# The output projection of feed-forward 1: the second pass begun within the first, and gated tiles loaded from ScalarE's queue

## The chip, the cores and the metric

The kernel runs on one core of one Trainium2 chip. The core has a matrix engine (TensorE, PE), a vector engine (VectorE, DVE), an engine for functions of one operand (ScalarE, ACT), GpSimd (POOL) and SyncE (SP), which here only issues DMAs; ScalarE can issue DMAs as well. The metric is the time of one execution on the device in microseconds, as the median of several runs.

## The reference

One layer works on 512 latent tokens and 256 context tokens of 1024 values, in float32. What matters here is the first of its two feed-forwards and the modulation rows:

```python
mod = (sc @ w_mod[l] + b_mod[l]).reshape(-1, N_MOD, D_MODEL)      # nine rows of 1024 per stream
x = ada_out(x, swiglu(ada_in(x, mod, 0, norm_pre[l, 0]), ffn_w_in[l, 0], ffn_w_out[l, 0]), mod, 0, norm_post[l, 0], 0.5)
xc = ada_out(xc, swiglu(ada_in(xc, modc, 0, ...), ...), modc, 0, norm_post[l, 0], 0.5)
# swiglu: a, b = split(y @ w_in); (silu(a) * b) @ w_out, with w_out of 2816 x 1024
# ada_out: x + 0.5 * gate * rmsnorm(z, g);  ada_in: rmsnorm(x, g) * (1 + scale) + shift
```

After it come a mixer (mLSTM heads and pooling) and a second feed-forward on the latent tokens alone, whose gate is row 8 of the modulation.

## The kernel before

Each float32 product is done as three matmuls: both operands are split into a high and a low part (`split_w`: the cast by ScalarE, line 81 by its helper, the difference by VectorE, line 78), and high x high, low x high and high x low are added in PSUM (`mm3`, lines 97 to 99; `mm3p`, line 102, the same in program order). Tokens are six tiles of 128: two of context, four latent. The hidden width of 2816 is 22 row blocks of 128.

The first half of feed-forward 1 (`in_fast`, one call per row block) makes the gated tile of 128 x 768 of each row block and stores it in DRAM (`g_d`). Its normed input lies in `yh` and `yl`.

The output projection (`out_pass`) takes two passes of three token tiles (384 tokens) each, so that its sums, three tiles x two halves of 512 columns, fit six PSUM banks: four of `pa`, two of `pz`. In a pass a row block needs its weights (512 KB, from `ffn_w_out` through the ring `raw` of five buffers, split into two `win` tiles) and its gated tile (192 KB, from `g_d`, split in `q3` buffers). `prepare` does both, two row blocks ahead, and all loads are issued by SyncE. The last row blocks (`tail`: 2 in the first pass, 4 in the second) go over one token tile after the other, so that each tile's end (`done1` and `ada_tile`: squares of the sums by ScalarE, line 148; the product with the gate row by VectorE, line 175, which empties the bank; the residual, line 179; the store of x1, line 185; a second norm, lines 148 and 187) lies beside the matmuls of the next. `back` then transposes the normed rows (line 105) and writes them, split, into `yh` and `yl`; `Backs(lag)` holds it back by so many ticks. The second pass goes through the row blocks with the last four of the first pass first, whose weight tiles are still there.

The other modulation rows (blocks 2 to 8) are made by `mod_steps`, a generator with ten steps per block: eight that each load one weight tile of 512 KB and add it, times a scalar, into a sum on VectorE (line 678, one operation per stream), one empty one, and one that sums over partitions on TensorE (line 688) and stores the row (line 704). `filler(n)` takes n steps. `in_fast` calls its `tick` twice per row block, and three of four ticks take one step (27 in all); the passes take the rest. When block 4 is done, `begin_chain` loads the gate rows and columns.

The order within each engine's queue is fixed when the program is built: a planner takes the instructions by priority and readiness, `keep_in_program_order` (`pin`) holds some of them in the order in which the code names them, and `issue_after` puts a group behind an instruction. An engine does its queue in order.

## Time and profile before

| | us |
|---|---|
| median of 3 runs | 1173.79 (1169.68 to 1174.12) |
| the profiled execution | 1170.85 |
| its span, first to last instruction | 1169.1 |
| TensorE busy in it | 1111.0 |
| VectorE busy in it | 894.8 |
| ScalarE busy in it | 530.6 |

All times of instructions below count from the first instruction of the profiled execution. The output projection lies at about 376 to 590 us, the first half of feed-forward 1 before it, the mixer at 620 to 825 and feed-forward 2 from 825 to the end.

### The profile page before, as it was taken

What the parts mean: (1) busy time and instruction counts of PE and PEld (TensorE: products, weight loads), DVE (VectorE), ACT (ScalarE), POOL (GpSimd) and SP (SyncE); (2) the same over time, 40 slices, a digit from 0 to 9 for tenths busy, and PEclk for the clock granted to TensorE, in tenths of its full rate; (3) what the DMA queues carried; (4) which work ended last, traced back from release to release, by engine and by line L of the source; (5) the groups of instructions that cost most, each with busy time, mean ns of one, the idle gap of its engine ahead of it and who ended that gap; (6) DMA issues with size and microseconds to landing.
All of it is one profiled execution on the core that took longest, in us unless ns stands there. A gap on an engine that the chain in (4) does not pass through costs nothing.

```text
span 1169.1 us, 17262 instructions
## 1 busy us (share of the span) xinstructions
PE 1111.0 (95%) x6610; PEld 1004.8 (86%) x6610; DVE 894.8 (77%) x1315; ACT 530.6 (45%) x910; POOL 106.4 (9%) x139
## 2 busy tenths in 40 slices
PE   4999999999999999599899799999999999999996
PEld 3899999999998877478699687888999899999995
DVE  3798997898798676557445867875899898888865
ACT  4544333333333333464364556557665344444431
POOL 4000000000000000200122314412000000000001
PEclk9999999999999999799999899999999999999999
DMA  9933433643544887549623112134334333333321
GB/s 306 287 121 104 151 124 100 200 133 97 184 153 127 328 301 274 190 159 324 215 83 99 37 63 64 64 109 148 123 91 120 116 108 109 109 108 109 107 75 73
DMA packets 152673, 169.25 MB, mean 145 GB/s; under 512 B 7415, under 2 KB 125687, under 8 KB 152589
## 3 DMA queue, kind: packets, MB, share of 16 engines
q1 hardware_dynamic: 152540, 168.12, 44.6%
q8 instruction: 52, 0.85, 0.3%
q14 instruction: 33, 0.26, 0.1%
q10 hardware_dynamic: 48, 0.01, 0.0%
HBM read 153.12 MB, written 14.98 MB: 144 GB/s over the span
## 4 chain that ended last, share of the span: by engine, by line
PE 47%; DVE 6%; ACT 2%; DMA 1%; issue 1%; POOL 1%; SPq 0%; DVEq 0%; ACTq 0%; POOLq 0%
PE pa L102 9%; PE pa L98 7%; PE pa L99 7%; PE pa L97 7%; PE pz L102 4%; PE pz L97 3%; PE pz L98 3%; PE pz L99 3%; PE pt L102 3%; PE pt L105 1%; DVE wins L78 1%; DMA raw<-in_w_in_dram 1%; ACT junk L148 1%; DMA q<-g 0%; DVE z L179 0%
## 5 line engine op out<-in xcount | busy, mean ns | idle before, releaser
L97 PE MATMUL pa<-yh,wins 128*128 128x256 f32 (+1 forms) x768 | 236.2, 308 | 0.7 <-ACT yh L81 0.4
L99 PE MATMUL pa<-yl,wins 128*128 128x256 f32 (+1 forms) x768 | 235.9, 307 | 0.0
L98 PE MATMUL pa<-yh,wins 128*128 128x256 f32 (+1 forms) x768 | 235.8, 307 | 0.0
L78 DVE TENSOR_TENSOR wins<-raw,wins 128x1024 fp32r<-128x1024 f32 (+1 forms) x144 | 156.6, 1087 | 70.5 <-PE pa L98 39.8
L81 ACT CAST wins<-raw 128x1024 fp32r<-128x1024 f32 (+1 forms) x146 | 136.2, 935 | 110.5 <-PE pa L99 36.9
L97 PEld LDWEIGHTS pa<-yh,wins 128*128 128x128 f32 x768 | 145.0, 189 | 3.0 <-issue 0.8
L99 PEld LDWEIGHTS pa<-yl,wins 128*128 128x128 f32 x768 | 144.9, 189 | 0.5
L98 PEld LDWEIGHTS pa<-yh,wins 128*128 128x128 f32 x768 | 144.9, 189 | 0.5
L99 PE MATMUL pa<-tl,wins 128*128 128x384 f32 (+1 forms) x388 | 122.3, 315 | 0.0
L98 PE MATMUL pa<-th,wins 128*128 128x384 f32 (+1 forms) x388 | 121.8, 314 | 0.0
L97 PE MATMUL pa<-th,wins 128*128 128x384 f32 (+1 forms) x388 | 121.3, 313 | 0.0
L678 DVE SCALAR_TENSOR_TENSOR m<-m,sc,m 128x1024 f32<-128x1024 f32 x80 | 100.2, 1278 | 9.6 <-DMA m<-in_w_mod_dram 5.9
L81 ACT CAST wins<-sw 128x1024 fp32r<-128x1024 f32 x78 | 81.7, 1047 | 48.9 <-PE pa L99 35.5
L78 DVE TENSOR_TENSOR wins<-sw,wins 128x1024 fp32r<-128x1024 f32 x78 | 95.2, 1221 | 10.7 <-PE pa L98 7.0
L102 PE MATMUL pa<-yh,wins 128*128 128x512 f32 (+2 forms) x352 | 97.0, 362 | 0.0
L97 PEld LDWEIGHTS pa<-th,wins 128*128 128x128 f32 x388 | 72.8, 188 | 0.9 <-issue 0.8
L99 PEld LDWEIGHTS pa<-tl,wins 128*128 128x128 f32 x388 | 73.0, 188 | 0.1
L98 PEld LDWEIGHTS pa<-th,wins 128*128 128x128 f32 x388 | 73.0, 188 | 0.0
L102 PEld LDWEIGHTS pa<-yh,wins 128*128 128x128 f32 x352 | 62.0, 191 | 9.2 <-issue 2.2
L97 PE MATMUL pa<-wins,q 128*128 128x512 f32 x148 | 55.3, 407 | 8.9 <-ACT q L81 8.9
L102 PE MATMUL pa<-yl,wins 128*128 128x512 f32 (+2 forms) x176 | 62.4, 355 | 0.5 <-DVE yl L78 0.5
L98 PE MATMUL pa<-wins,q 128*128 128x512 f32 x148 | 59.3, 400 | 1.2 <-DVE q L78 1.2
(388 smaller groups left out, 2177.1 us busy)
## 6 DMA issues: line engine op xcount, KB each, us to landing
raw<-in_ffn_w_in_dram SPq DMA_DIRECT2D x87, 512.0 KB
raw<-in_ffn_w_out_dram SPq DMA_DIRECT2D x62, 512.0 KB
m<-in_w_mod_dram SPq DMA_DIRECT2D x57, 512.0 KB
g<-q SPq DMA_DIRECT2D x22, 384.0 KB
q<-g SPq DMA_DIRECT2D x44, 192.0 KB
raw<-in_w_in_dram SPq DMA_DIRECT2D x16, 512.0 KB
raw<-in_w_mod_dram SPq DMA_DIRECT2D x11, 512.0 KB
raw<-in_w_out_dram SPq DMA_DIRECT2D x16, 256.0 KB
```

Source lines behind the costliest of these rows:

```text
L78: return eng.tensor_tensor(out=out_ap, in0=a, in1=b, op=ALU.subtract)
L81: return S.copy(hi, src)
L97: T.matmul(out_ap, lhsT=wh, rhs=xh, start=first, stop=False, **kw)
L98: T.matmul(out_ap, lhsT=wl, rhs=xh, start=False, stop=False, **kw)
L99: T.matmul(out_ap, lhsT=wh, rhs=xl, start=False, stop=last, **kw)
L102: return tc.keep_in_program_order(T.matmul(*args, **kw))
L105: return tc.keep_in_program_order(T.transpose(**kw))
L148: return S.activation(out=junk, in_=src, func=AF.Square, scale=D ** -0.5, accum_out=ssq)
L678: V.scalar_tensor_tensor(out=accs[st], in0=w, scalar=sc[:, st * KD + k:st * KD + k + 1], in1=accs[st], op0=ALU.mult, op1=ALU.add)
```

## The change

- `out_pass` becomes a class. `fetch` loads a gated tile, from ScalarE's queue, and is pinned; `prepare` loads and splits the weights and splits the gated tile. Tiles are fetched five to six row blocks ahead and prepared two ahead, as before.
- `first.start(1)` prepares the first row block before the last call of `in_fast`. `second.start(4)` fetches and prepares four row blocks of the second pass after the last row block of the first pass is prepared and before its tail.
- The second pass multiplies its first four row blocks (`head`) for one token tile after the other.
- Ten weight tiles are kept for the second pass: four in `win` as before, six more in the space of `yh` and `yl`, which is free until `back` writes. For that the ticks by which `back` is held rise from 4 to 14. The second pass starts with these ten.
- The store of x1 and those of the modulation rows are issued by ScalarE; the store in `ada_tile` comes after the square of the second norm.
- `mod_steps` takes its blocks and buffers as arguments, and loads the norm's gains ahead of the weights of a block. From the 17th tick on every tick of `in_fast` takes a step (32 steps in all); the first pass takes one in every second row block, the second one in each of its first 18.
- Block 8 is made in feed-forward 2, one step per call of `in_fast` there, with `raw` buffers for its weights.

```diff
--- before.py
+++ after.py
@@ -166,7 +166,7 @@
     x1_d = [dpool.tile([P, D], F32, name=f"x1_{t}") for t in range(4)]
     x2_d = [dpool.tile([P, D], F32, name=f"x2_{t}") for t in range(4)]
 
-    def ada_tile(t, zs, z, halves, xr, gc, store, nxt, junk, half, keep=lambda ins: ins):
+    def ada_tile(t, zs, z, halves, xr, gc, store, nxt, junk, half, keep=lambda ins: ins, put=load):
 
 
         r = rstd2(halves)
@@ -181,9 +181,9 @@
                 load(store[:, cs], z[:, cs])
         if nxt is None:
             return None
+        r2 = rstd1(z, junk)
         if store is not None:
-            load(store, z)
-        r2 = rstd1(z, junk)
+            put(store, z)
         V.tensor_scalar_mul(xr, z, r2)
         scale, shift = nxt
         ts = slice(t * P, (t + 1) * P)
@@ -386,7 +386,9 @@
             qd = pa()
             product(qd, uh[:, lo], ul[:, lo], "t3")
             V.tensor_add(u3, u2, qd[:, 0:n])
-            self.tick(V.tensor_add(cb[:, n:2 * n], u3, p5))
+            end = V.tensor_add(cb[:, n:2 * n], u3, p5)
+            if self is f1:
+                self.tick(end)
             qe = pa()
             product(qe, x22p[:, lo], x22p[:, hi], "t4")
             V.tensor_add(cb[:, 0:n], u3, qe[:, 0:n])
@@ -472,7 +474,7 @@
             st = 1 if t < 2 else 0
             load(xr, ctxt[t * P:(t + 1) * P, :] if t < 2 else x[(t - 2) * P:(t - 1) * P, :])
             return ada_tile(t, qs, z, halves, xr, chain["g"][st], None if t < 2 else x1_d[t - 2], chain["y"][st], junk,
-                            lambda: q3()[:, 0:512], pin)
+                            lambda: q3()[:, 0:512], pin, nc.scalar.dma_start)
 
         blocks1 = ((0, 384), (384, 384))
         f1 = Ffn(ffn_w_in[0], ffn_w_out[0], range(NTT), 0, NT)
@@ -664,47 +666,53 @@
             S.mul(wqk, kc(p), float(P) ** -0.5)
 
 
-        def mod_steps():
-            for blk, streams in ((2, (0, 1)), (3, (0, 1)), (4, (0, 1)), (5, (0,)), (6, (0,)), (7, (0,)), (8, (0,))):
+        def mod_steps(blocks, new, acc, ahead):
+            for blk, streams in blocks:
                 accs = {}
+                j, ty = divmod(blk, 3)
+
+                nq = 4 // len(streams)
+                n = D // nq
+                at = [(st, i, 32 * (nq * st + i), slice(i * n, (i + 1) * n)) for st in streams for i in range(nq)]
+
+                def gains():
+                    gb = new()[:, 0:n]
+                    src = norm_pre if ty == 1 else norm_post
+                    for st, i, g, cs in at:
+                        load(gb[g:g + 32], src[j:j + 1, cs].broadcast_to([32, n]))
+                    return gb
+
                 for st in streams:
-                    accs[st] = m4()
+                    accs[st] = acc()
                     G.memset(accs[st], 0.0)
                     load(accs[st][0:1, :], b_mod[blk:blk + 1, :])
+                res = gains() if ty and ahead else None
                 for k in range(KD):
-                    w = m4()
+                    w = new()
                     load(w, w_mod[k * P:(k + 1) * P, blk * D:(blk + 1) * D])
                     for st in streams:
                         V.scalar_tensor_tensor(out=accs[st], in0=w, scalar=sc[:, st * KD + k:st * KD + k + 1],
                                                in1=accs[st], op0=ALU.mult, op1=ALU.add)
                     yield
                 yield
-
-                nq = 4 // len(streams)
-                n = D // nq
-                at = [(st, i, 32 * (nq * st + i), slice(i * n, (i + 1) * n)) for st in streams for i in range(nq)]
                 p = pt()[:, 0:n]
...
-                res = m4()[:, 0:n]
                 if ty == 0:
+                    res = new()[:, 0:n]
                     S.copy(res, p)
                 else:
-                    gb = m4()[:, 0:n]
-                    src = norm_pre if ty == 1 else norm_post
-                    for st, i, g, cs in at:
-                        load(gb[g:g + 32], src[j:j + 1, cs].broadcast_to([32, n]))
-                    V.scalar_tensor_tensor(out=res, in0=p, in1=gb, op1=ALU.mult,
+                    res = res if ahead else gains()
+                    V.scalar_tensor_tensor(out=res, in0=p, in1=res, op1=ALU.mult,
                                            **(dict(scalar=1.0, op0=ALU.add) if ty == 1 else
                                               dict(scalar=1.0 if j == 1 else 0.5, op0=ALU.mult)))
                 for st in streams:
                     rows[(blk, st)] = dpool.tile([1, D], F32, name=f"row{blk}_{st}")
                 for st, i, g, cs in at:
-                    load(rows[(blk, st)][:, cs], res[g:g + 1])
+                    nc.scalar.dma_start(rows[(blk, st)][:, cs], res[g:g + 1])
                 yield blk
 
-        steps = mod_steps()
+        steps = mod_steps([(b, (0, 1)) for b in (2, 3, 4)] + [(b, (0,)) for b in (5, 6, 7)], m4, m4, True)
 
         def filler(n):
             for _ in range(n):
@@ -734,67 +742,110 @@
         count = iter(range(100))
 
         def mod_tick(ins):
-            if next(count) % 4 < 3:
+            i = next(count)
+            if i % 4 < 3 or i > 16:
                 with tc.issue_after(ins.ins):
                     filler(1)
 
         f1.tick = mod_tick
-        for f in range(4, NF):
-            f1.in_fast(f)
-
 
         wos = {}
 
-        def out_pass(half, order, tail, homes, z, xr, before, backs):
...
+        class OutPass:
+            def __init__(self, half, order, head, tail, homes):
+                self.half, self.order, self.head, self.tail, self.homes = half, order, head, tail, homes
+                self.g, self.raws = {}, {}
+
+            def fetch(self, f):
+
+                self.raws[f] = q3()[:, 0:384]
+                pin(nc.scalar.dma_start(self.raws[f], g_d[f][:, 384 * self.half:384 * self.half + 384]))
+
+            def prepare(self, f):
                 if f not in wos:
                     r = raw()
                     load(r, f1.wo_ap[f * P:(f + 1) * P, :])
...
+                    wos[f] = split_w(r, to=self.homes[f]() if f in self.homes else None, keep=pin)
                 g = q3(F32R)
...
+                self.g[f] = split_w(self.raws[f], to=(g[:, 0:384], g[:, 384:NT]), keep=pin)
+
+            def start(self, n):
+
+                self.loaded, self.ready = iter(self.order), iter(self.order)
+                for f in self.order[:n]:
+                    self.fetch(next(self.loaded))
+                for f in self.order[:n]:
+                    self.prepare(next(self.ready))
+                self.n = n
+
+            def more(self, i):
+                if i + 5 >= self.n:
+                    for f in [next(self.loaded, None) for _ in range(max(1, 6 - self.n if i == 0 else 1))]:
+                        if f is not None:
+                            self.fetch(f)
+                if i + 2 >= self.n:
+                    for f in [next(self.ready, None) for _ in range(3 - self.n if i == 0 else 1)]:
+                        if f is not None:
+                            self.prepare(f)
+
+            def product(self, f, j, h, mm3):
+                (gh, gl), (wh, wl) = self.g[f], wos[f]
+                ts, cs = slice(j * P, (j + 1) * P), slice(512 * h, 512 * h + 512)
+                mm3(self.qs[j][h], gh[:, ts], gl[:, ts], wh[:, cs], wl[:, cs], f == self.order[0], f == self.order[-1])
+
+            def run(self, z, xr, before, backs, fill, then=lambda: None):
+                order, head, tail = self.order, self.head, self.tail
+                self.qs = [(pa(), pa()), (pa(), pa()), (pz(), pz())]
+                for i in range(head):
+                    self.more(i)
+                for j in range(3):
+                    for f in order[:head]:
+                        for h in range(2):
+                            self.product(f, j, h, mm3)
+                for i in range(head):
+                    before.tick()
+                for i, f in enumerate(order[:-tail]):
+                    if i >= head:
+                        self.more(i)
+                        for j in range(3):
+                            for h in range(2):
+                                self.product(f, j, h, mm3)
+                        before.tick()
+                    filler(fill(i))
+                for i in range(len(order) - tail, len(order)):
+                    self.more(i)
+                then()
+                for j in range(3):
+                    t, halves = 3 * self.half + j, small(2)
                     for h in range(2):
...
+                        for f in order[-tail:]:
+                            self.product(f, j, h, mm3p)
+                        square_to(halves[:, h:h + 1], self.qs[j][h], junk[:, 512 * h:512 * h + 512])
+                        backs.tick()
+                    backs.add(done1(t, self.qs[j], z[:, j], halves, xr(j)))
 
...
-        backs, first_backs = Backs(4), Backs(4)
+        first = OutPass(0, list(range(NF)), 0, 2, {0: lambda: (m4(F32R), m4(F32R))})
+        for f in range(4, NF):
+            if f == NF - 1:
+                first.start(1)
+            f1.in_fast(f)
+
+        backs, first_backs = Backs(4), Backs(14)
         xr1 = rows3("tl")
         order = list(range(NF))
-        out_pass(0, order, 2, {0: lambda: (sw(F32R), sw(F32R))}, rows3("th"), lambda i: xr1[:, i], Backs(0), first_backs)
-        for f in order[:-4]:
+
+        kept = order[-10:-4]
+        places = [y.rearrange("p k c -> p (k c)")[:, i * D:(i + 1) * D] for i in range(6) for y in (yh, yl)]
+        homes = {f: lambda i=i: (places[2 * i], places[2 * i + 1]) for i, f in enumerate(kept)}
+        first.homes.update(homes)
+        order = order[-10:] + order[-11::-1]
+        second = OutPass(1, order, 4, 4, {})
+        first.run(rows3("th"), lambda i: xr1[:, i], Backs(0), first_backs, lambda i: i % 2, lambda: second.start(4))
+        for f in order[10:]:
             wos.pop(f)
-        order = order[-4:] + order[-5::-1]
         homes = {order[-4]: lambda: (sw(F32R), sw(F32R))}
         late = []
 
@@ -805,7 +856,8 @@
             return late.pop(0)
 
         homes.update({order[-3]: late_home, order[-2]: late_home})
-        out_pass(1, order, 4, homes, rows3("tl"), lambda i: m4(), first_backs, backs)
+        second.homes.update(homes)
+        second.run(rows3("tl"), lambda i: m4(), first_backs, backs, lambda i: 1)
 
 
         wv = []
@@ -1317,13 +1369,23 @@
         pool = sx.enter_context(tc.tile_pool(name="ffn2", bufs=6, reuse_waits="tile"))
         sums = sx.enter_context(tc.tile_pool(name="sums2", bufs=1, reuse_waits="tile"))
         junk = pool.tile([P, D], BF16, name="junk3", bufs=1)
-        gc2 = pool.tile([P, D], F32, name="gc2", bufs=1)
-        bc_row(gc2, (8, 0))
+
+        def row_tile():
+            return pool.tile([P, D], F32, tag="gc2", name="gc2", bufs=1)
+
+        late = mod_steps([(8, (0,))], raw, row_tile, False)
+        gains2 = []
+
+        def last_row(ins):
+            if not gains2:
+                with tc.issue_after(ins.ins):
+                    if next(late, None) == 8:
+                        gains2.append(bc_row(row_tile(), (8, 0)))
 
         def done2(t, z, halves):
             xr = raw()
             load(xr, x2_d[t - 2])
-            return ada_tile(t, [z[:, 0:512], z[:, 512:1024]], z, halves, xr, gc2, out[(t - 2) * P:(t - 1) * P, :], None, junk, None)
+            return ada_tile(t, [z[:, 0:512], z[:, 512:1024]], z, halves, xr, gains2[0], out[(t - 2) * P:(t - 1) * P, :], None, junk, None)
 
         f2.scope(pool, done2, lambda: None, junk)
 
@@ -1352,7 +1414,7 @@
         f2.wo = {f: f2.out_weights(f, f) for f in range(2)}
         f2.w[2] = f2.last_sums(first)
         rest()
-        f2.fast = True
+        f2.fast, f2.tick = True, last_row
         f2.run(lambda f: ((NCTX, NLAT),), started=(0, 1))
```

## Rows read from the trace of the kernel before

**Rows 1.** The page: busy us, share of the span and instructions of each engine.
```profile
PE 1111.0 (95%) x6610; PEld 1004.8 (86%) x6610; DVE 894.8 (77%) x1315; ACT 530.6 (45%) x910; POOL 106.4 (9%) x139
```

**Rows 2.** Busy us by stretch (counts), then TensorE's clock, DMA share and GB/s.
```profile
376.00:575.00 199.00, 180.88 (x799) 142.97 (x799) 126.51 (x144) 82.79 (x136) 12.46 (x22) 0.95 0.73 259
465.00:470.00 5.00, 4.83 (x15) 3.87 (x16) 2.55 (x4) 1.38 (x4) 0.39 (x2) 0.67 1.02 401
480.00:485.00 5.00, 0.00 (x0) 0.00 (x0) 4.26 (x7) 4.07 (x10) 1.64 (x4) 0.50 0.04 14
485.00:490.00 5.00, 3.16 (x7) 2.05 (x8) 3.14 (x4) 1.10 (x4) 2.07 (x3) 0.50 0.92 274
505.00:555.00 50.00, 50.00 (x227) 40.28 (x226) 33.99 (x38) 26.25 (x41) 0.00 (x0) 1.00 0.80 279
```

**Rows 3.** Timeline, TensorE, second pass: start, us, engine, line, operation.
```profile
546.59 0.39 PE L97 MATMUL pa<-wins,q 128*128 128x512 f32 x1
554.81 0.39 PE L97 MATMUL pa<-wins,q 128*128 128x512 f32 x1
```

**Rows 4.** Timeline, first pass's tail: start, us; in brackets idle before, releaser.
```profile
461.31 0.85 PE L102 MATMUL pa<-wins,q 128*128 128x512 f32 x3
462.35 1.05 ACT L81 CAST wins<-raw 128x1024 fp32r<-128x1024 f32 x1 [3.70 <-DMA raw<-in_ffn_w_out_dram]
465.18 6.30 PE L102 MATMUL pa<-wins,q 128*128 128x512 f32 x20 [0.81 <-DVE q L78]
471.31 2.94 PE L102 MATMUL pz<-wins,q 128*128 128x512 f32 x12
```

**Rows 5.** Timeline, seam between the passes.
```profile
476.12 0.63 PE L105 MATMUL pt<-ident,tlz 128*128 128x128 f32 x4 [1.87 <-DVE tlz L187]
481.41 1.28 DVE L175 TENSOR_TENSOR thz<-pz,m 128x512 f32<-128x512 f32 x2
484.03 0.34 SPq L185 DMA_DIRECT2D x<-thz  x1
484.48 0.38 SPq L759 DMA_DIRECT2D q<-g  x1
485.10 0.50 ACT L81 CAST q<-q 128x384 fp32r<-128x384 f32 x1
485.64 1.65 PE L97 MATMUL pa<-wins,q 128*128 128x512 f32 x3 [8.90 <-ACT q L81]
492.35 0.40 PE L97 MATMUL pz<-wins,q 128*128 128x512 f32 x1
```

**Rows 6.** Timeline, second pass's tail; last row from the chain of work.
```profile
561.41 0.34 SPq L759 DMA_DIRECT2D q<-g  x1
563.74 0.51 ACT L81 CAST q<-q 128x384 fp32r<-128x384 f32 x1 [9.25 <-DMA q<-g]
568.01 0.84 PE L102 MATMUL pa<-sw,q 128*128 128x512 f32 x3
584.79 5.48 PE pz L102 x24
```

**Rows 7.** Two lines' instructions: least, median, most ns, and starts.
```profile
L678 DVE SCALAR_TENSOR_TENSOR m<-m,sc,m x80: 1272/1278/1285, 112.8 to 541.6; 128x1024 f32<-128x1024 f32 x80
L759 SPq DMA_DIRECT2D q<-g x44: 319/384/1433, 362.6 to 564.3; - x44
```

**Rows 8.** Busy time by stretch, two row blocks of feed-forward 1's first half.
```profile
141.00:155.70 14.70, 14.70 (x86) 14.70 (x85) 14.56 (x19) 5.64 (x9) 0.00 (x0) 1.00 0.43 134
155.70:170.40 14.70, 14.70 (x86) 14.70 (x85) 12.12 (x17) 5.59 (x9) 0.00 (x0) 1.00 0.37 117
```

**Rows 9.** Busy time by stretch, feed-forward 2; SyncE's waits 850:1000 (us, times, longest).
```profile
850.10:936.90 86.80, 85.32 (x612) 80.11 (x611) 81.70 (x123) 42.92 (x65) 0.00 (x0) 1.00 0.36 108
936.90:1029.70 92.80, 92.80 (x650) 87.05 (x650) 79.95 (x122) 40.05 (x61) 0.00 (x0) 1.00 0.36 107
SPq L114 <- DVE wos L78: 43.2, 9, 11.3
```

More of the change, by code (lines that the diff above doesn't have):

```diff
@@ L768, in out_pass @@
-            for f in order[:2]:
-                prepare(f)
-            for f, later in zip(order[:-tail], order[2:]):
-                prepare(later)
-                for i in range(3):
-                    for h in range(2):
-                        product(f, i, h, mm3)
-                before.tick()
-                filler(2 if half == 0 and f % 3 == 0 else 1)
-            for f in order[len(order) - tail + 2:]:
-                prepare(f)
-            for i in range(3):
-                t, halves = 3 * half + i, small(2)
-                for h in range(2):
-                    for f in order[-tail:]:
-                        product(f, i, h, mm3p)
-                    square_to(halves[:, h:h + 1], qs[i][h], junk[:, 512 * h:512 * h + 512])
-                    backs.tick()
-                backs.add(done1(t, qs[i], z[:, i], halves, xr(i)))
+                self.g[f] = split_w(self.raws[f], to=(g[:, 0:384], g[:, 384:NT]), keep=pin)
```

13 lines of the change are left out of this document (removed).

## Prediction

> **What bounds the kernel now.** I read the page's busy times first. TensorE is busy for 1111.0 of 1169.1 us [rows 1], so almost all of the time is matmuls that the change doesn't remove, and only the 58 us in which TensorE is idle, and the stretches at a low clock, can be won. The granted clock and the busy time by stretch come next. The output projection of feed-forward 1 lies at 376 to about 590 us; in its first 199 us TensorE is busy for 180.88, at a mean clock of 0.95 of full speed, and around it there are long stretches without any idle time. Last I read the order of time around each hole. There are three, and each can be priced against the undisturbed pace: 36 matmuls of 512 columns lie between the starts 546.59 and 554.81, so one takes 0.228 us [rows 3].
>
> **Hole A, the tail of the first pass.** It runs from 461.31 to 474.25 (471.31 + 2.94), 12.9 us for 3 tiles x 2 halves x 2 row blocks x 3 = 36 matmuls, which at 0.228 are 8.2 us. Lost: 4.7 us. The wait is for a split on ScalarE that itself waited for a weight load (3.70 us, released by the DMA) [rows 4]; the clock then reads 0.67 in 465 to 470, between its two levels of 1.2 and 2.4 GHz, after the idle time [rows 2].
>
> **Hole B, the seam between the passes.** From 474.25 to 492.35, 18.1 us, TensorE does four transposes (0.6) and 12 matmuls (2.7). Lost: 14.8 us. The reader is to see a chain of queues: SyncE issues the store of the first latent tile (x<-thz) only at 484.03, and the next load of a gated tile (q<-g) only right behind it at 484.48; ScalarE's first split for the new pass is at 485.10, and TensorE, idle for 8.90 us, starts at 485.64 [rows 5]. DMA share in 480 to 485 is 0.04, so nothing is short of bandwidth there; and in 485 to 490 the clock is 0.50, its lower level, after those 9 us without a matmul [rows 2].
>
> **Hole C, the tail of the second pass.** From 568.01 to 590.27 (584.79 + 5.48), 22.3 us for 3 x 2 x 4 x 3 = 72 matmuls, which are 16.4 us. Lost: 5.8 us. The load of a late gated tile is issued at 561.41 only, and ScalarE has stood idle for 9.25 us when it arrives [rows 6].
>
> A + B + C = 25.3 us. This is what the change can win.
>
> **The change part by part.**
>
> Gated tiles through ScalarE's queue, five to six row blocks ahead, and the store of x1 and of the modulation rows there as well. This takes out of SyncE's queue just the store that held the load at 484.48. The 44 loads cost SyncE 0.384 us each in the median, at most 1.43 [rows 7]; ScalarE now pays that. In 505 to 555, twelve row blocks of 4.1 us, ScalarE is busy for 26.25 of 50 us, so 2.2 per row block, with 1.9 free [rows 2]; 0.38 fits. Bounds: from nothing to 1.43 per row block, which still fits. I take nothing. What is queued behind an issue on ScalarE are the casts of the following weights and tiles, two row blocks (8 us) ahead of TensorE.
>
> Here the Trainium skill speaks against the change. Its page "DMA: Bandwidth & Descriptors", section "Issuing engines are not separate DMA queues", says that transfers started from different engines end on the same 16 DMA engines and interleave, so that spreading them saves issue time alone. By it, hole B would stay but for issue time; the share of 0.04 in the hole says that B is order, not bandwidth, so there I go by the row. For A and C it is the first rival.
>
> Second pass begun tile by tile. The first four row blocks of the second pass are loaded and split before the first pass's tail, and are multiplied for one token tile after the other: 24 matmuls, 5.5 us, for each tile. The third tile's banks come free last, at 482.69 (481.41 + 1.28), 8.4 us after the tail's end; before, each row block went over all three tiles, so the first one already needed them. Now they are needed only after 11 us. VectorE is freer in this stretch too, since fewer modulation steps lie in it. So B goes, but for a margin of 2.6 us that I don't trust fully: residue 1 us, bounds 0 and 7.4 (half of it).
>
> Ten weight tiles kept instead of four. The second pass loads and splits 12 instead of 18 blocks of 512 KB. Of the modulation loads, 8 remain in the first pass (21 before) and 14 in the second (12 before), counted from the steps. Over the stage that is 17 loads, 8.9 MB, less than the 51.5 MB (259 GB/s x 199 us [rows 2]) of now, and 6.8 MB of it leave the first pass, at whose end hole A is a late load. A goes; of C I leave 2 us, as a row's store now waits in ScalarE's queue shortly before the last splits (bounds 0 and 5.8).
>
> The y tiles of the first three token tiles are written later, after the kept weights in their place were used; transposes and casts are the same in number and lie beside matmuls. Free.
>
> More modulation steps in feed-forward 1's first half (32 instead of 27). Five steps of two VectorE operations of 1.278 us [rows 7] are 12.8 us on VectorE. A row block with two of them per tick pair (four operations) has VectorE at 14.56 of 14.70 us, one with two operations at 12.12, and TensorE at 14.70 in both [rows 8]. So a full row block fits, with 0.14 us to spare, but so far every second one was a light one; now three and then four full ones follow each other. Bounds 0 and 12.8; I take 0.5, as the nearest row shows no wait at the same load.
>
> The last gate row (block 8) moves into feed-forward 2: eight weight tiles of 512 KB through the ring of five raw buffers, and eight operations of 1.28 us on VectorE, one per row block from 850 us on. From 850.1 to 936.9 VectorE is busy for 81.70 of 86.80 us: 5.1 us free, and seven operations are 8.9 us, so 3.8 are missing; from there on it has 12.8 us free in 92.8 [rows 9]. SyncE already waits long for raw buffers there (43.2 us in nine waits for one line alone) [rows 9]. Even at this load TensorE was busy for 85.32 of the 86.80 us, so VectorE has some lead and part of the lack is hidden. Bounds 0 and 10.2 (all eight on the path); I take 3. What is late next is the split of the next row block's weights, which queues behind the new operation, and TensorE waits for that. The skill's page "Perfetto Trace Analysis", section "Identifying the Most-Contended Engine", takes occupancy as a fair measure of how near VectorE is to its limit; with 94% in the row it names VectorE as the engine to spare here. By that rule all that is missing, 3.8 us, would show, instead of the 3 I take.
>
> **Sum.** The profiled execution took 1170.85 us (span 1169.1). 1170.85 - 25.3 + 1 (B) + 2 (C) + 0.5 + 3 = 1152.1. That execution lies 2.9 us below the median of the three runs (1173.79) and inside their range; a median of the changed kernel may lie as much above it, so I put 1153.
>
> **Rivals.**
>
> First: the tails are short of bandwidth, and the queue doesn't matter. For it: DMA share 1.02 in 465 to 470 [rows 2]. Against: holes at 0.04. Then A and C shrink only with the bytes, by 17%: of 10.5 us 8.7 stay. 1170.85 - 14.8 - 1.8 + 1 + 3.5 = 1158.8. Chance 0.15.
>
> Second: the seam doesn't close, the change doesn't do there what it says. ScalarE's queue is in order, and the four early tiles' splits may stand in it behind the squares of the first pass's last tiles, or the third tile's banks come more than 2.6 us later than before. Then half of B stays: 1170.85 - 25.3 + 7.4 + 2 + 3.5 = 1158.5. Chance 0.14.
>
> Third: feed-forward 2 pays in full, and the ring of raw buffers with it: 10.2 instead of 3, so 1159.3, and with a late load for every third row block of about 2 us some 1165. For it: the 94% above. Against: after 936.9 VectorE has room. Chance 0.10.
>
> Fourth, on the other side: ScalarE is held by the loads that it now issues. A load that has to wait for its buffer or for a place in the queue stops the casts behind it. From 1.9 us per row block it stretches the row block of 4.1 us; at 2.3 us on each of 44 the 18.7 us of the sum are gone, at 2.8 it costs 44 x 0.9 = 40 us, so 1152.1 + 40 = 1192. For it: one issue took 1.43 us. Against: the median of 0.384, and ten buffers for some eight tiles alive. Chance 0.05.
>
> **How the numbers follow.** Forecast 0.54, the four rivals 0.15, 0.14, 0.10 and 0.05; 0.02 for several of the costs together that leave no change. About 0.5% (5.9 us) is what a measurement of this kernel can tell from none. Faster by more than that, below 1167.9: forecast, first and second rival, and most of the third, 0.88, less 0.02 for their upper ends, 0.86; within it 0.08; slower 0.06. The range: at the low end all 25.3 us are won and nothing is paid, 1145.5, and 1 us for the runs, so 1144; at the high end the first three rivals with their outer ends, 1165.
>
> **What would show it.** In the trace after: no idle time above 1 us and a clock of 1.0 between the last tail matmul of the first pass and the second pass; tail matmuls at 0.23 us in both tails; loads q<-g in ScalarE's queue and no stretched ScalarE; TensorE fully busy from 230 to 370; 0 to 4 us of waits for VectorE in the first eight row blocks of feed-forward 2. I would be wrong if holes of the same sum appear elsewhere, or if a full row block of feed-forward 1 grows beyond 14.7 us.

## The result, and the profile after

The changed kernel takes 1159.83 us (median of 4 runs, 1159.06 to 1162.81), the kernel before 1172.84 us beside it: a ratio of 0.9898, 95% interval 0.987 to 0.9925. The profiled execution took 1160.3 us, with a span of 1158.6; before it was 1170.85 and 1169.1.

The page of the changed kernel, busy us, share of the span and instructions (as [rows 1]):

```profile
PE 1107.9 (96%) x6610; PEld 1002.4 (87%) x6610; DVE 886.3 (76%) x1309; ACT 522.9 (45%) x904; POOL 104.6 (9%) x139
```

The number of matmuls is the same; the span is 10.5 us shorter. To see where, I cut both executions at the same five instructions: the tick (line 379) of row block 19 of feed-forward 1, the first matmul of the first tail, that of the second tail, the first matmul after the projection, and the first and last tick of feed-forward 2. All times in us:

| stretch | before | after | change |
|---|---|---|---|
| start to the tick of row block 19 | 335.64 | 336.54 | +0.9 |
| to the first tail | 125.67 | 128.63 | +3.0 |
| first tail and second pass | 106.70 | 86.59 | -20.1 |
| second tail | 22.45 | 22.47 | 0.0 |
| mixer, to feed-forward 2's first tick | 259.62 | 260.41 | +0.8 |
| feed-forward 2, first to last tick | 282.38 | 286.32 | +3.9 |
| to the end | 36.64 | 37.64 | +1.0 |

The gain lies in one row, holes A and B; 4.7 us of it are hole A, as the first tail now takes 8.2 us (465.17 to 473.41) instead of 12.9. Hole C stayed, a new hole came ahead of the first tail, and feed-forward 2 grew.

**The seam.** Busy time by stretch after (columns as in [rows 2]), and the matmuls and the third tile's banks there:

```profile
473.40:480.00 6.60, 6.60 (x31) 5.46 (x30) 4.18 (x7) 2.89 (x8) 2.43 (x6) 1.00 0.01 1
480.00:490.00 10.00, 10.00 (x46) 8.28 (x45) 5.45 (x8) 3.14 (x6) 2.26 (x5) 1.00 0.55 174
```

```profile
465.17 5.66 PE L102 MATMUL pa<-wins,q 128*128 128x512 f32 x24
...
473.41 0.39 PE L97 MATMUL pa<-yh,q 128*128 128x512 f32 x1
...
479.75 1.28 DVE L175 TENSOR_TENSOR thz<-pz,m 128x512 f32<-128x512 f32 x2
...
482.53 0.33 ACTq L186 DMA_DIRECT2D x<-thz  x1
482.89 1.31 ACTq L762 DMA_DIRECT2D q<-g  x2
```

Where [rows 5] had 8.90 us without a matmul, the second pass now follows the tail at its own pace, with kept weights from the space of `yh`, at a clock of 1.00. The store of x1 still waits for the third tile, and a load still stands right behind it, now on ScalarE; but the tiles that the second pass begins with were loaded and split long before.

**Ahead of the first tail.** VectorE, TensorE and one issue of SyncE around the fifth row block of the first pass (18 matmuls each; the expectation below calls it the fourth):

```profile
389.48 1.28 DVE L694 SCALAR_TENSOR_TENSOR m<-m,sc,m 128x1024 f32<-128x1024 f32 x1 [2.16 <-issue]
390.79 2.16 SPq L692 DMA_DIRECT2D m<-in_w_mod_dram  x2
...
396.25 1.28 DVE L694 SCALAR_TENSOR_TENSOR m<-m,sc,m 128x1024 f32<-128x1024 f32 x1 [3.66 <-DMA m<-in_w_mod_dram]
398.59 0.55 DVE L78 TENSOR_TENSOR q<-q,q 128x384 fp32r<-128x384 f32 x1
399.19 0.50 PE L98 MATMUL pa<-wins,q 128*128 128x512 f32 x1 [2.65 <-DVE q L78]
```

VectorE stands 3.66 us for a modulation weight; the splits that TensorE needs are behind it in its queue. SyncE issued the load of that weight only at 390.79, as the addition of 389.48 ended and gave its buffer back, and VectorE could start on it 5.5 us later. TensorE also waits 1.32 us, at 372.02, for the first gated tile's cast. Before, the same start had cost 0.56 us.

**The second tail.** ScalarE, TensorE and VectorE:

```profile
544.55 0.51 ACT L81 CAST q<-q 128x384 fp32r<-128x384 f32 x1
...
551.19 0.64 PE L700 MATMUL pt<-m,ones 128*32 128x256 f32 x8
551.89 0.43 DVE L706 SCALAR_TENSOR_TENSOR m<-pt,m 128x256 f32<-128x256 f32 x1 [5.02 <-PE pt L700]
552.35 1.18 ACTq L712 DMA_DIRECT2D row<-m  x4
553.58 1.04 ACT L81 CAST w<-raw 128x1024 fp32r<-128x1024 f32 x1 [8.52 <-DMA row<-m]
555.09 0.49 PE L102 MATMUL pa<-w,q 128*128 128x512 f32 x1 [1.67 <-ACT q L81]
```

ScalarE did its last cast at 544.55 and then stood for 8.5 us before the store of block 7's row, which needs the product of VectorE, which needs eight matmuls that stand behind the 18th row block. The casts for the tail are behind that store. In the first pass ScalarE stood longer still for the store of block 5's row, and VectorE for weights about as long as above:

```profile
447.35 1.29 DVE L694 SCALAR_TENSOR_TENSOR m<-m,sc,m 128x1024 f32<-128x1024 f32 x1 [3.69 <-DMA m<-in_w_mod_dram]
...
450.64 1.05 ACT L81 CAST wins<-raw 128x1024 fp32r<-128x1024 f32 x1 [18.05 <-DMA row<-m]
```

TensorE has no pause from 400 us to the first tail: there it had enough split operands ahead. So the length of such a wait doesn't tell its cost.

**Feed-forward 1 and 2.** A row block with four modulation operations in feed-forward 1 (as [rows 8]), then feed-forward 2 from its first tick, two stretches of six row blocks each (as [rows 9]):

```profile
246.99:261.74 14.75, 14.75 (x85) 14.75 (x85) 14.57 (x19) 5.64 (x9) 0.96 (x1) 1.00 0.31 99
...
834.64:922.71 88.07, 86.49 (x612) 80.50 (x611) 85.30 (x125) 40.47 (x64) 0.00 (x0) 1.00 0.46 135
922.71:1018.03 95.32, 94.21 (x658) 87.35 (x657) 85.15 (x129) 41.53 (x63) 0.00 (x0) 1.00 0.44 129
```

In feed-forward 1 VectorE is at 99% and TensorE never stops: from row block 3 to 19 it takes 238.88 us before and after. In feed-forward 2 the first six row blocks, with six additions of block 8, grew by 1.3 us against [rows 9], the next six, with the last two additions, the row's sum and its store, by 2.5, and the rest hardly.

### The profile page after: what moved, and what is told of

It reads as the page before. It is cut to its first block, busy times and chain, and to the rows that moved or that the text cites. A ratio compares the mean times of both kernels' runs of the same rounds, so it can differ in the third digit from the quotient of the medians.

```text
span 1158.6 us, 17190 instructions
## 1 busy us (share of the span) xinstructions
PE 1107.9 (96%) x6610; PEld 1002.4 (87%) x6610; DVE 886.3 (76%) x1309; ACT 522.9 (45%) x904; POOL 104.6 (9%) x139
## 4 chain that ended last, share of the span: by engine, by line
PE 76%; DVE 9%; DMA 6%; ACT 3%; issue 2%; POOL 1%; ACTq 0%; SPq 0%; DVEq 0%; POOLq 0%
PE pa L98 16%; PE pa L99 16%; PE pa L97 15%; PE pa L102 10%; PE pz L102 5%; PE pz L97 4%; DMA m<-in_w_mod_dram 3%; PE pz L98 3%; PE pz L99 3%; PE pt L102 3%; DVE wins L78 1%; DVE m L694 1%; PE pt L105 1%; ACT junk L148 1%; DMA raw<-in_w_mod_dram 1%
## 5 line engine op out<-in xcount | busy, mean ns | idle before, releaser
L78 DVE TENSOR_TENSOR wins<-raw,wins 128x1024 fp32r<-128x1024 f32 (+1 forms) x132 | 141.6, 1074 | 60.2 <-ACT wins L81 31.1
L81 ACT CAST wins<-raw 128x1024 fp32r<-128x1024 f32 (+1 forms) x134 | 123.0, 925 | 100.4 <-PE pa L99 35.0
L694 DVE SCALAR_TENSOR_TENSOR m<-m,sc,m 128x1024 f32<-128x1024 f32 x72 | 90.1, 1279 | 25.4 <-DMA m<-in_w_mod_dram 22.0
L97 PE MATMUL pz<-wos,gh 128*128 128x512 f32 x144 | 56.6, 393 | 1.6 <-DVE z L429 1.1
L98 PE MATMUL pz<-wos,gl 128*128 128x512 f32 x144 | 56.3, 391 | 0.0
```

Source lines behind the costliest of these rows:

```text
L78: return eng.tensor_tensor(out=out_ap, in0=a, in1=b, op=ALU.subtract)
L81: return S.copy(hi, src)
L97: T.matmul(out_ap, lhsT=wh, rhs=xh, start=first, stop=False, **kw)
L98: T.matmul(out_ap, lhsT=wl, rhs=xh, start=False, stop=False, **kw)
L694: V.scalar_tensor_tensor(out=accs[st], in0=w, scalar=sc[:, st * KD + k:st * KD + k + 1], in1=accs[st], op0=ALU.mult, op1=ALU.add)
```

## Experiments

Each is the changed kernel with the edit shown, if nothing else is said. The stretches are cut as above.

| | to the first tail | first tail, second pass | second tail | feed-forward 2 |
|---|---|---|---|---|
| before | 125.67 | 106.70 | 22.45 | 282.38 |
| after | 128.63 | 86.59 | 22.47 | 286.32 |
| rows stored by SyncE | 130.83 | 86.58 | 18.48 | 286.49 |
| gated tiles by SyncE | 134.66 | 86.59 | 22.45 | 287.27 |
| head 0 | 129.30 | 88.88 | 21.66 | 286.49 |
| before, with ScalarE's queue alone | 140.05 | 106.80 | 20.73 | 282.04 |
| second pass prepared after the tail | 128.36 | 106.94 | 23.02 | 286.73 |
| four tiles kept | 129.80 | 86.92 | 22.71 | 287.34 |
| block 8 back in the passes | 132.59 | 87.44 | 23.23 | 282.63 |
| no steps in four first row blocks | 124.79 | 90.99 | 22.43 | 286.73 |
| steps moved | 125.29 | 86.72 | 16.79 | 287.73 |
| steps moved, block 8 later | 125.47 | 86.73 | 16.78 | 284.03 |

**What closed the seam.** Three runs take the parts apart. First, the second pass prepared after the first pass's tail:

```diff
-        first.run(..., lambda i: i % 2, lambda: second.start(4))
+        first.run(..., lambda i: i % 2)
 ...
+        second.start(4)
         second.run(...)
```

> The changed kernel with the second pass's first four row blocks fetched and split only after the first pass's tail in the program, everything else as changed. Theory: the splits must stand ahead of the tail's squares and products; else they come 8 us or more after the tail and the second pass takes 5 to 10 us longer than the 78.4 us of the changed kernel. Rival: going tile by tile hides the seam by itself, since the planner moves the splits forward anyway; then within 2 us.

1181.61 us in one run, against 1175.86 of before beside it. ScalarE, its DMA queue and TensorE in the seam:

```profile
483.06 0.35 ACTq L186 DMA_DIRECT2D x<-thz  x1
483.45 1.27 ACTq L762 DMA_DIRECT2D q<-g  x2
...
486.80 0.51 ACT L81 CAST q<-q 128x384 fp32r<-128x384 f32 x1 [2.64 <-DMA q<-g]
487.37 1.22 PE L97 MATMUL pa<-yh,q 128*128 128x512 f32 x2 [12.70 <-ACT q L81]
```

The whole 20 us come back, more than expected. The loads stand behind the store of x1 here, the first cast waits for its load, and TensorE for the cast. The theory holds; the rival falls.

Second, the kernel before with ScalarE's queue alone:

```diff
-                load(r, g_d[f][:, c0:c0 + 384])
+                nc.scalar.dma_start(r, g_d[f][:, c0:c0 + 384])
```

(and the x1 store by `put`, as in the change).

> The kernel before with one part of the change alone: the 44 gated tiles and the three x1 stores are issued by ScalarE, at the same places in the program. Theory that the banks set the seam: hole B shrinks only until the third tile's banks are free, from 14.8 us to 10 to 12, and the time by 2 to 5 us. Rival, the queue is the whole of it: B falls below 5 us and the time by about 10 us. Third: ScalarE's queue is in order as well and its loads stand behind squares; then the seam stays as it is or grows.

1184.62 us in one run, against a median of 1171.41 of before. The seam still costs 8.90 us without a matmul, and the first pass is 14 us longer. Who ScalarE waited for from 376 to 500 us (us in all, times, longest), and the seam:

```profile
ACT q L81 <- DMA q<-g: 58.4, 20, 5.8
```

```profile
491.69 0.33 ACTq L759 DMA_DIRECT2D q<-g  x1
...
495.67 1.06 ACT L148 ACTIVATE junk<-thz 128x1024 bf16<-128x1024 f32 x1 [0.90 <-DVE thz L179]
496.73 0.49 ACT L81 CAST q<-q 128x384 fp32r<-128x384 f32 x1
497.27 0.80 PE L97 MATMUL pa<-wins,q 128*128 128x512 f32 x1 [8.90 <-ACT q L81]
```

The third expectation holds. ScalarE waits 20 times for a load that it issued itself just before. That is a form of the fourth rival of the prediction (the cast right behind an issue waits for the landing), and it makes the kernel slower where the loads aren't issued ahead.

That the 8.90 us are the same in both kernels corrects the prediction's reading of hole B. The same place in the kernel before:

```profile
474.49 0.42 SPq L759 DMA_DIRECT2D q<-g  x1
...
484.04 1.06 ACT L148 ACTIVATE junk<-thz 128x1024 bf16<-128x1024 f32 x1 [0.90 <-DVE thz L179]
...
487.67 0.51 ACT L81 CAST q<-q 128x384 fp32r<-128x384 f32 x1 [2.08 <-DMA q<-g]
488.49 0.80 PE L98 MATMUL pa<-wins,q 128*128 128x512 f32 x1 [1.20 <-DVE q L78]
```

The cast at 485.10 ([rows 5]) waits for no load: its tile was loaded from 474.49 on, ahead of the store. It stands in ScalarE's queue behind the square of the third tile (line 148), which waits for VectorE's end of that tile, as the cast at 496.73 does with the other queue. The load at 484.48, behind the store, is that of the second row block: the cast that waits for it is the next one, at 487.67. TensorE's one further wait, at 488.49, is for a difference that VectorE does right behind the third tile's second norm (487.90). So hole B is the order within the queues of the two computing engines, and the load behind the store cost at most a small part of it.

Third, the other way round: the early loads, but from SyncE's queue.

```diff
-                pin(nc.scalar.dma_start(self.raws[f], g_d[f][...]))
+                pin(load(self.raws[f], g_d[f][...]))
```

> The changed kernel with the gated tiles loaded from SyncE's queue again, at the same places in the program, so still five to six row blocks ahead. Theory that the queue matters: SyncE waits for the buffers of modulation weights, the gated tiles stand behind that, and holes of 2 to 6 us in all come back in the two passes. Rival, the rule that the issuing queue saves issue time alone: the two passes take what they take in the changed kernel, within 1 us, and the early fetch is what closed the holes.

This run took 2217.15 us, with every matmul from the first stretch on at twice its time, far from the edit, too; it tells nothing of the edit, so the kernel was run again:

> The same kernel as in the second experiment, whose only run went at half pace from its first matmul on: the changed kernel with the gated tiles loaded from SyncE's queue, still five to six row blocks ahead. The rows of that slow run showed no wait of TensorE beyond one of 6 us, which is a hint only. Theory that the queue matters: holes of 2 to 6 us in all more than in the changed kernel, in the two passes. Rival, the queue saves issue time alone: the two passes within 1 us of the changed kernel.

1166.18 us. First pass and second pass differ. SyncE and TensorE at the first pass's start, and the same loads in the changed kernel:

```profile
382.06 0.84 SPq L692 DMA_DIRECT2D m<-in_w_mod_dram  x2
382.96 2.94 SPq L762 DMA_DIRECT2D q<-g  x5
389.81 0.80 PE L97 MATMUL pa<-wins,q 128*128 128x512 f32 x1 [7.55 <-ACT q L81]
```

```profile
377.67 3.29 ACTq L762 DMA_DIRECT2D q<-g  x5
```

One hole of 7.55 us at the first pass's start, where the loads go out 5.3 us later, behind two modulation weights; 6.0 us more in that stretch; the seam, the second pass and the second tail as in the changed kernel, to 0.1 us. So the queue is worth 6 us at the start of the first pass and nothing at the seam, which the early loads and splits close by themselves. The holes were expected in both passes; there is one.

**The banks.** The second pass begun over all three tiles:

```diff
-        second = OutPass(1, order, 4, 4, {})
+        second = OutPass(1, order, 0, 4, {})
```

> The changed kernel with the second pass begun row block by row block over all three token tiles (head 0 instead of 4); the four early row blocks are still prepared before the first pass's tail. Theory that the banks set the seam: the third tile's banks come free about 8 us after the tail, TensorE can do two tiles of one row block (2.7 us) or, as planned, some more, and stands for about 5 us, with a low clock after it: 5 to 8 us longer than the changed kernel. Rival: hole B was late splits alone, which the early preparation cures; then it is within 1 us of the changed kernel.

1161.9 us in one run; the seam stretch is 2.3 us longer. TensorE:

```profile
480.83 0.50 PE L97 MATMUL pz<-yh,q 128*128 128x512 f32 x1 [1.57 <-DVE thz L175]
```

It waits for the third tile's banks, as the theory says, but for 1.57 us, not 5: the planner put the matmuls of two row blocks on the first two tiles, 5.5 us, ahead of it. Both expectations are off in size. Going tile by tile is worth about 2 us, the early preparation some 20.

**The kept tiles.** Four instead of ten:

```diff
-        kept = order[-10:-4]
+        kept = []
-        order = order[-10:] + order[-11::-1]
+        order = order[-4:] + order[-5::-1]
-        for f in order[10:]:
+        for f in order[4:]:
```

> The changed kernel with four weight tiles kept instead of ten (order and release of the second pass follow). Theory: the six loads and splits less are bandwidth and VectorE's time that nothing waits for, so the second pass takes 78 to 80 us as in the changed kernel and the time is within 2 us of it. Rival: without them the second pass's start has to load weights while the tail of the first is running, holes come back and it takes 3 to 8 us longer.

1161.15 us in one run, each stretch within 1.2 us of the changed kernel. Nothing waited for those six loads and splits.

**The second tail.** Rows stored by SyncE again:

```diff
-                    nc.scalar.dma_start(rows[(blk, st)][:, cs], res[g:g + 1])
+                    load(rows[(blk, st)][:, cs], res[g:g + 1])
```

> The changed kernel with one line undone: the modulation rows are stored from SyncE's queue again, not from ScalarE's. Theory: hole C, 5.7 us lost in the tail of the second pass, stayed because ScalarE stands for 8.5 us before the store of block 7's row, with the casts of the last weights and gated tiles behind it. Then the tail of 72 matmuls takes 17 to 19 us instead of 22.1 and the time falls by 3 to 5 us, to about 1156. Rival: those casts wait for late loads of weights, whoever issues the store; then the tail stays at 21 to 23 us and the time at about 1160. Second rival: SyncE is held in ScalarE's place and the weights of the mixer come late; then the tail is short and the time is lost in the 20 us after it.

1157.86 us, ratio 0.9878 (0.9843 to 0.9913); the interval overlaps that of the changed kernel, so the verdict is the stretch: the tail takes 18.48 instead of 22.47 us. What is left of the hole is VectorE, which waits for the same eight matmuls:

```profile
553.09 0.43 DVE L706 SCALAR_TENSOR_TENSOR m<-pt,m 128x256 f32<-128x256 f32 x1 [5.02 <-PE pt L700]
...
555.17 0.72 PE L102 MATMUL pa<-w,q 128*128 128x512 f32 x2 [0.34 <-DVE q L78]
```

The theory holds, and the second rival doesn't show (the mixer stretch takes 260.91 us, 260.41 in the changed kernel). The first stretch is 2.2 us longer; its waits are of the same size, but the granted clock fell after them (0.83 in 370 to 380, 0.86 in 400 to 410), where it stayed at 1.00 in the changed kernel.

**The first pass's start.** No modulation steps in its first four row blocks:

```diff
-  lambda i: i % 2                     lambda i: 1
+  lambda i: int(i % 2 and i > 3)      lambda i: 2 if i < 2 else 1
```

(fill of the first and of the second pass)

> The changed kernel without modulation steps in the first four row blocks of the first pass; its two steps go to the first two row blocks of the second pass. Theory: the hole of 2.65 us in the first pass's fourth row block is VectorE standing 3.7 us for a modulation weight, with the split of the next weights behind it; then the stretch from the last full row block of feed-forward 1 to the first tail falls from 128.6 to about 126 us. Rival: the weights of that row block come late because six gated tiles are fetched at once; then the hole stays, within 1 us.

1159.15 us in one run. The hole is gone (124.79 us), so it was VectorE before a modulation weight and not the six early tiles. The steps moved in the program more than in time: VectorE still does additions at 388.32, 390.66 and 395.53, but now the splits go ahead of them (first two lines). The two steps put at the second pass's start cost 4.4 us there, since VectorE has to empty the banks at that time; the clock, too, reads 0.83 in 466 to 476:

```profile
395.06 0.55 DVE L78 TENSOR_TENSOR q<-q,q 128x384 fp32r<-128x384 f32 x1
395.53 1.28 DVE L694 SCALAR_TENSOR_TENSOR m<-m,sc,m 128x1024 f32<-128x1024 f32 x1
...
466.41 1.28 DVE L694 SCALAR_TENSOR_TENSOR m<-m,sc,m 128x1024 f32<-128x1024 f32 x1 [2.98 <-DMA m<-in_w_mod_dram]
...
469.88 0.50 PE L97 MATMUL pa<-yh,q 128*128 128x512 f32 x1 [1.07 <-DVE thz L175]
```

**Feed-forward 2.** Block 8 made in the passes again, ten steps more in the first:

```diff
-        steps = mod_steps([...] + [(b, (0,)) for b in (5, 6, 7)], m4, m4, True)
+        steps = mod_steps([...] + [(b, (0,)) for b in (5, 6, 7, 8)], m4, m4, True)
-        f2.fast, f2.tick = True, last_row
+        f2.fast = True
```

(first pass: fill 1; the last gate row loaded at the start of feed-forward 2)

> The changed kernel with block 8 of the modulation put back into the two passes (one step in every row block of the first pass instead of every second one) and nothing added to feed-forward 2. Theory: the 3.9 us by which feed-forward 2 grew, from the first to the last tick 286.3 instead of 282.4 us, are VectorE's additions and the weight loads of block 8; then that stretch falls back to 282 to 283 us, and the passes grow by 0 to 4 us as their loads do. Rival: the stretch grew for another reason (the order that the planner chose, or when it starts), and stays at 285 to 287.

1159.54 us in one run: feed-forward 2 is back at 282.63, and the stretch to the first tail grew by 4.0, by the same hole as above, now 5.2 us long. The theory holds for feed-forward 2. The passes grew by 5.6 us with the seam and the second tail, more than the 0 to 4 expected, so the time as a whole is no better.

**A better version.** From the last three: the steps where neither VectorE's splits, nor the banks, nor the row's store are in a hurry.

```diff
-  lambda i: i % 2                     lambda i: 1
+  lambda i: int(4 < i < 19)           lambda i: 0 if i < 4 or i > 13 else 2 if i < 8 else 1
```

> The changed kernel with its modulation steps in other row blocks: first pass none in the first five and one in each of the 14 after; second pass none in the first four, two in each of the next four, one in the six after, so that block 7 ends four row blocks ahead of the tail. Stores stay on ScalarE's queue. Theory: hole at the first pass's start and hole in the second tail are both a matter of where these steps stand (VectorE before a weight load, ScalarE before a row's store). Then the stretch to the first tail takes about 125 us (128.6), the second tail 17 to 19 (22.5), the seam stays closed (first tail and second pass together 86 to 88), and the time falls by 5 to 8 us to about 1153. Rival: with the steps elsewhere the same waits come elsewhere, and the four stretches together stay within 2 us of the changed kernel's 237.7.

1150.57 us, ratio 0.9812 (0.9798 to 0.9825), a little more than the 5 to 8 us expected. The second tail takes 16.79 us for its 72 matmuls, with the stores still on ScalarE's queue: a row's store whose data comes early costs nothing there; only with late data was the queue worth 4.0 us (above). And, on top of that, block 8's steps six row blocks later (`calls` counts the ticks):

```diff
-            if not gains2:
+            if next(calls) > 5 and not gains2:
```

> The same, and in feed-forward 2 the steps of block 8 begin six row blocks later, where VectorE had 12.8 us free in 92.8 before the change. Theory: the 3.9 us there are VectorE's lack in the first row blocks; the stretch from the first to the last tick falls from 286.3 to 283 to 284 us, and the time to about 1150. Rival: it is the ring of raw buffers, which is as full later on; then the stretch stays at 285 to 287.

1146.56 us, ratio 0.9781 (0.9767 to 0.9796). Feed-forward 2 from its first tick, cut at the same ticks as above, with the seven row blocks after them as a third stretch, and the changed kernel's third stretch below:

```profile
824.26:910.00 85.74, 85.05 (x612) 80.04 (x611) 80.76 (x122) 43.03 (x65) 0.00 (x0) 1.00 0.37 111
910.00:1002.94 92.94, 92.94 (x651) 87.03 (x650) 84.66 (x126) 38.80 (x61) 0.00 (x0) 1.00 0.44 134
1002.94:1108.29 105.35, 104.18 (x743) 97.38 (x742) 91.14 (x137) 46.39 (x71) 0.00 (x0) 1.00 0.42 127
...
1018.03:1120.96 102.93, 102.93 (x735) 97.12 (x734) 87.07 (x131) 45.84 (x70) 0.00 (x0) 1.00 0.35 108
```

The first six row blocks are back, at 85.7 us. The next six now hold six additions and take 92.9 us, where [rows 9] has 92.8 without any, with VectorE at 91% and TensorE without a pause. The last seven, with the other two additions, the row's sum and its store, took 2.4 us more than in the changed kernel, where that end of block 8 lay in the second stretch, which grew by 2.5 instead. So the expected number came, 284.03, but VectorE's lack was the smaller part: most of the cost goes with the end of the block, wherever it stands. VectorE's waits for an input weight move with it (us in all, times, longest; the changed kernel from 834 to 1020 us, this version from 1002.94 to 1108.29):

```profile
DVE sw L343 <- DMA raw<-in_ffn_w_in_dram: 2.9, 2, 2.4
...
DVE sw L343 <- DMA raw<-in_ffn_w_in_dram: 4.4, 3, 1.9
```

Whether it is the raw buffers that are short there isn't settled.

## Why the prediction was right, and where it was off

The direction and the range were right: 1159.83 lies between 1144 and 1165. The point of 1153 was too low; for the profiled execution the sum said 1152.1 and it took 1160.3.

- **Holes A and B**: forecast 18.5 us won, measured 20.1. The price of the holes against the undisturbed pace was right, and that the order of queues makes them, not bandwidth. But neither chain was the one that I read. For B I took the load behind the store of x1 for what holds the first split; it was the square of the third tile ahead of it in ScalarE's queue (the same 8.90 us with the loads on the other queue). The early preparation puts loads and splits ahead of both, so that the number came out all the same is in part luck. For A I counted on the modulation loads that leave the first pass, 8 left of 21; in the trace 16 of these additions still run before the first tail, 18 before the change. The rows that I passed over show SyncE before the change, which issued nothing from 439.07 to 451.35:

```profile
SPq L704 <- ACT m L692: 11.4, 1, 11.4
...
451.35 1.12 SPq L704 DMA_DIRECT2D row<-m  x4
...
455.15 0.51 SPq L756 DMA_DIRECT2D raw<-in_ffn_w_out_dram  x1
```

SyncE waited 11.4 us for the store of a modulation row, and the weight that the tail waits for went out only behind it. Which part of the change closed A no run isolates: the first tail takes 8.2 to 8.3 us also with the rows stored by SyncE, with the gated tiles loaded by SyncE, with four tiles kept and with block 8 back. The two margins that I put at B, banks and splits, weren't needed; the second rival's loss, and more, is what the later preparation showed.
- **Hole C**: forecast 3.8 of 5.8 us won, measured none. The step is the one that left 2 us because a row's store waits in ScalarE's queue ahead of the last splits. The mechanism was named; its size was guessed. The row for it was there: the load at 561.41 in [rows 6] stands right behind the store of such a row, for which SyncE had waited 5.9 us, and VectorE before it for the eight matmuls:

```profile
SPq L704 <- DVE m L698: 5.9, 1, 5.9
...
559.79 0.43 DVE L698 SCALAR_TENSOR_TENSOR m<-pt,m 128x256 f32<-128x256 f32 x1 [6.34 <-PE pt L688]
```

The change moved the store, and its wait with it, to ScalarE.
- **The start of the first pass**: taken as free, measured +3.0 us. I counted the modulation loads that leave the first pass, wrongly as said, and not where the remaining ones stand. Of the ring of six buffers the gate rows, the sum and the gains loaded ahead leave two for weights, so a load waits for the last addition but one: the one for 396.25 went out at 390.79. Six gated tiles and several weights are on their way at the same time (DMA share 0.97 in 390 to 400). The run without these steps shows that the split behind VectorE's wait is the cost; how much of the 5.5 us from the issue to the addition that traffic makes stays open.
- **Feed-forward 1**: forecast 0.5, measured 0.0, at 99% of VectorE in its full row blocks. A row that shows the load that is to come, and no wait, was a good bound. The added work was less than the 12.8 us of the sum: from row block 3 to 19 VectorE is busy for 212.04 instead of 205.51 us, and at 376 us 48 additions are done in both kernels. Of the five steps two have no addition, and two belong to a block with one stream.
- **Feed-forward 2**: forecast 3, measured 3.9, of which the 0.6 us of eight matmuls only changed place. The sum has a miscount: the 86.80 us of [rows 9] hold six row blocks, so six operations, 7.7 us, and 2.6 us are missing, not 3.8. The Trainium skill's rule in "Perfetto Trace Analysis", section "Identifying the Most-Contended Engine", takes occupancy as the measure; as the prediction used it, all 2.6 us would show in these six row blocks. They grew by 1.3, so the trace agrees in direction and not in size. The other 2.5 us came in the next six row blocks, where VectorE is at 89%, and go with the end of block 8, as the last version shows. That 3.9 lies near 3.8 is luck.
- **The first rival**, bandwidth at the tails, is out: the first tail takes 8.24 us, and the second 16.8 in the better version. The Trainium skill's "DMA: Bandwidth & Descriptors", section "Issuing engines are not separate DMA queues", says that spreading saves issue time alone. The run with the gated tiles on SyncE agrees for the seam and the second pass, and differs at the first pass's start by 6.0 us. There it isn't speed of transfer that the queue gives, but what stands ahead of the load.
- **The fourth rival**, ScalarE held by what it issues, happened in other forms. In the changed kernel the stores of rows held it, for 8.5 us in the second tail, which cost hole C, and for 18.05 us in the first pass, which cost nothing. In the kernel before with that queue alone its casts waited for its own loads all along the first pass.
- Start, mixer and end add 2.7 us in the profiled execution. In the other executions the tick of row block 3 comes between 96.5 and 98.5 us, the mixer takes 259.6 to 260.9 and the end 36.5 to 37.7, with the same code there; this part I don't explain further.

## What to carry to other kernels

A load, a split or a cast that stands behind something that waits is late, on whatever queue. Load and split the first operands of the next phase ahead of the waits that end this one, and put a store where its data is already there: on an engine that computes, a waiting store cost 4.0 us more here than on SyncE. Before naming what held an operand, look which load its cast needs; two issues that stand close together in the rows are not yet a cause. Background work belongs in row blocks where neither operands for the next matmuls nor full banks wait for the same engine, and its place is worth as much as its amount: here 9 us for the same steps in other row blocks. When a stage is prepared early, look for what its first row blocks now share with the stage that ends.

## What was not expected of the hardware

VectorE at 14.57 of 14.75 us per row block, several in a row, didn't slow TensorE at all, while one wait of 3.66 us for a load cost it 2.65 us, and a wait of 3.69 us for the same kind of load, 51 us later, nothing. And after waits of TensorE of 1.69 and 2.04 us the clock fell to 0.83 and 0.86 in one run, while after 1.32 and 2.65 us it stayed at 1.00 in another: the same holes cost 2 us more or less.
